# One hybrid layer on one core: the RWKV chain's solve taken tokens-first, its rounds regrouped, attention buffers freed sooner, x loaded in longer rows

## The chip, the cores and the metric

The kernel runs on one core of a Trainium2 chip. The metric is the device time of one execution in microseconds (us), the median of several runs. A profile is one further execution, recorded instruction by instruction.

## What is computed

The reference is one layer of a hybrid network on 256 tokens of width 2048, all in float32:

```python
h = rms_norm(x, norm_g)
proj = h @ w_in                      # 2048 -> 20672 columns, cut into the parts below
y_a = attention(q_a, k_a, v_a, rel_bias) * silu(z_a)         # 12 heads of 128, causal, T5 bias
y_b = rwkv7_time_mix(r_b, k_b, v_b, lw, la, ...) * silu(z_b) # 24 heads of 64
y_c = memory_cross_attention(q_c, mem_n, w_mem_kv) * silu(z_c)
merged = g_a*(y_a @ w_proj_a) + g_b*(y_b @ w_proj_b) + g_c*(y_c @ w_proj_c)
out = rms_norm(x + merged @ w_out, final_norm_g)
```

The time mix keeps a 64x64 state per head and steps through the tokens:

```python
sa = einsum('bhvk,bhk->bhv', state, a_t)
state = state * w_t + sa[..., None] * b_t + v_t[..., None] * k_t
y_t = einsum('bhvk,bhk->bhv', state, r_t)
```

The kernel takes it in two chunks of 128 tokens: with the decays folded into the vectors, a chunk needs four 128x128 products of tokens with tokens (its grams, masked), the inverse of a unit triangular 128x128 matrix, and a few small matmuls with the state.

## The kernel before, in words

**The main stream.** The program walks a list of jobs, one per 256 or 512 output columns of a weight matrix. A job is cut into steps of four (or two, for the 512 wide ones) slices of 128 input rows. For each step a 512 KB piece of the weight is loaded into `raw` (`issue_dma`, L259, three buffers, on SP's queue), split into a high and a low part in `wt` by ACT (L270) and DVE (L273), and multiplied on PE: 16 matmuls of 512 and 256 columns (L308, L309) or 12 of 512 columns (L306). These are the main matmuls; their results stand in the four PSUM tiles `pm`.

**The lanes.** All else (the time mix, attention, the norms) is written as generators. After each step of the main stream `step_lanes` lets every lane go on to its next `yield`, so a lane's instructions stand between two steps on every engine, and `yield 2` leaves a step out. Engines execute in this written order. A lane waits for another by `wait(key)`, which only costs it steps. `force(key)` in a job's evacuation, and `drain()` at the end of a phase, run the lanes with no main matmuls between them. Lanes use four other PSUM tiles, `psd`, in turn: a fifth use waits until the first has been read.

**One pair of the time mix.** The 24 heads go in six groups g of four heads. `pairs_lane(g)` computes decay and gate (L521, L528), waits for R and K, builds the vectors `AR` and `BK`, turns sg and R to tokens on PE for the norms (L589), then waits for V and turns V and BK (L601 to L603) into `tok`. It starts `rw_lane(g)`, which computes the grams `GS` in four rounds (L623, masked by DVE at L627 and L628), sends the diagonal blocks through DRAM and back (`d1`, L660 and L669, both on SP's queue), inverts them on DVE (L680, L684), completes the inverse `XF` on PE (L715 to L745), and then for each chunk forms the input `W` of the inverse (`from_v` L640 and L643, `turn_a` L651), applies it (L762), updates the state S (L770, L771) and gives the output YT (L779, L780). The rest of the lane normalises: YT is turned on PE (L791), mean and difference are taken by DVE from PSUM (L794 to L800), and the result Y is turned back (L828).

**Attention A.** `attn_a(g)` loads the bias by way of DRAM rows (`spread_rows`, L421, on ACT's queue: `fr<-fd`), computes scores (L847, L849), the softmax, transposes of it (L876) and the product with V (L883, L885). `keep_evac`, which stores the next pair's q and k, forces the whole of the pair before.

**The start and the joint.** x is loaded in eight pieces of 256 KB on two queues; `x_stats` sums squares of each quarter on ACT and DVE while PE turns the identity (L915). After the last job of the time mix `open_p2` drains the lanes, gives their memory back and loads the second input `mem` (L981).

Of the kernel before, what the change touches and what calls it, by code (L numbers as in the profile page):

```python
# [38 lines left out]
def tile_hybrid(ctx: ExitStack, tc: tile.TileContext, x, mem, rel_bias, norm_g, mem_norm_g, w_in,  # L39
# [443 lines left out]
    def keep_evac(nm, g):  # L483
        def f(_):
            if g:
                force(("attn", g - 1))
# [19 lines left out]
    def pairs_lane(g):  # L506
# [17 lines left out]
        yield 1  # L524
# [58 lines left out]
        yield 1  # L583
        for t, o in ((sq, nb), (r, bs)):
# [8 lines left out]
        yield 1  # L593
        yield from wait(("V", g))
        yield 1
# [16 lines left out]
    def rw_lane(g, AR, BK, tok, nb, bs, esc):  # L612
        rw, GS, XF, X64 = (E[k] for k in ("rw", "GS", "XF", "X64"))
        if g:
            yield from wait(("state_free", g - 1))
        for c in range(2):
            for q in range(2):

                pv = [ps_side().rearrange("p (w x t) -> p w x t", w=2, x=2) for h in range(2)]
                for w in range(2):  # L620
                    for h in range(2):
                        rows = slice(64 * h, 64 * h + 64)
# [6 lines left out]
                yield 1  # L629
        flags["gram", g] = True  # L630
        S = E["S"]
        halves = [slice(64 * h, 64 * h + 64) for h in range(2)]

        def from_v(c, AY):
# [12 lines left out]

        def turn_a(AY, W):
            p = ps_side()
            for q in range(2):  # L650
                pe.transpose(p[:, q * 128:q * 128 + 128], AY[:, q, 0], ident)  # L651
            act.activation(W[:, 0], p[:, 0:256].rearrange("p (i v) -> p i v", i=4), AF.Copy)
# [6 lines left out]
        for d, s in enumerate(D4):  # L659
            nc.sync.dma_start(d1[d].rearrange("u s t -> s u t"), GS[s, :, 0, s])  # L660
        NB = rw.tile([128, 32, 32], FT, name="NB")
# [9 lines left out]
        for c in range(31, 0, -1):  # L671
# [15 lines left out]
            if c == 16:  # L687

                if g:
                    yield from wait(("pair_free", g - 1))  # L690
                AY0 = rw.tile([128, 2, 2, 128], FT, name="AY0", tag="Yq")
                from_v(0, AY0)
            if c == 8:
                W = rw.tile([128, 2, 4, 64], FT, name="W")
                turn_a(AY0, W)
# [23 lines left out]
        for s in D4[0:2]:  # L719
            act.activation(X64[s, :, s], XN[s], AF.Copy)  # L720
        yield 1
# [26 lines left out]

        Tt = rw.tile([128, 2, 2, 2, 128], FT, name="Tt", tag="NB")
        AY1, YT = Tt[:, 0], Tt[:, 1]  # L750
        for c in range(2):
            AY = (AY0, AY1)[c]
            if c:
                from_v(1, AY)
                yield 1
                W = rw.tile([128, 2, 4, 64], FT, name="W")
                turn_a(AY, W)
# [31 lines left out]
        for c in range(2):  # L789
            for q in range(2):  # L790
                pe.transpose(p[:, c * 256 + q * 128:c * 256 + q * 128 + 128], YT[:, c, q], ident)  # L791
# [516 lines left out]
```

## Time and profile before

| what | value |
|---|---|
| median of 3 runs | 1486.32 us (1486.04 to 1487.34) |
| the profiled execution's own time | 1486.92 us |
| its span, first to last instruction | 1485.2 us |
| PE busy over the span | 1453.7 us, 98% |
| DVE, ACT, POOL busy | 64%, 51%, 12% |
| PE busy in 0 to 40 us | 30.90 us |
| PE busy in 700 to 800 us | 93.01 us |
| PE busy in 1400 to 1485 us | 77.31 us |

The span is 1.7 us shorter than the execution's own time, which has the launch around it. Matmuls overlap in the pipeline, so a matmul's own duration is longer than the distance to the next start; what a group costs is read from start to start, or from the group's busy time. "Idle before" is the time in which an engine had nothing in flight, with what ended it.

### The profile page before, as it was taken

What the parts mean: (1) busy time and instruction counts of PE and PEld (TensorE: products, weight loads), DVE (VectorE), ACT (ScalarE), POOL (GpSimd) and SP (SyncE); (2) the same over time, 40 slices, a digit from 0 to 9 for tenths busy, and PEclk for the clock granted to TensorE, in tenths of its full rate; (3) what the DMA queues carried; (4) which work ended last, traced back from release to release, by engine and by line L of the source; (5) the groups of instructions that cost most, each with busy time, mean ns of one, the idle gap of its engine ahead of it and who ended that gap; (6) DMA issues with size and microseconds to landing.
All of it is one profiled execution on the core that took longest, in us unless ns stands there. A gap on an engine that the chain in (4) does not pass through costs nothing.

```text
span 1485.2 us, 22008 instructions
## 1 busy us (share of the span) xinstructions
PE 1453.7 (98%) x8219; PEld 1212.2 (82%) x8219; DVE 944.5 (64%) x1871; ACT 752.4 (51%) x1127; POOL 179.9 (12%) x252
## 2 busy tenths in 40 slices
PE   7999999999999999999899999999999999999997
PEld 6877878888888888788688888888888888888887
DVE  5667678687787688694557555655545545544555
ACT  6535545556456456455655545544443443444443
POOL 5211201313212224102100000000000000000011
PEclk9999999999999999999999999999999999999999
DMA  6655556456555465466556555566555565555753
GB/s 178 182 166 165 161 151 173 144 149 177 145 168 167 133 181 169 136 174 181 143 172 197 169 171 164 166 198 195 185 190 192 185 194 189 186 196 186 266 196 133
DMA packets 208544, 258.88 MB, mean 174 GB/s; under 512 B 28236, under 2 KB 146660, under 8 KB 207796
## 3 DMA queue, kind: packets, MB, share of 16 engines
q1 hardware_dynamic: 202160, 247.11, 54.4%
q10 hardware_dynamic: 4452, 6.71, 1.3%
q0 software_dynamic: 1824, 3.65, 0.9%
q8 instruction: 65, 1.06, 0.3%
q14 instruction: 43, 0.35, 0.1%
HBM read 253.74 MB, written 6.05 MB: 175 GB/s over the span
## 4 chain that ended last, share of the span: by engine, by line
PE 85%; DVE 5%; DMA 4%; ACT 3%; issue 1%; SPq 1%; POOL 0%; ACTq 0%; DVEq 0%; POOLq 0%
PE pm L306 43%; PE pm L308 22%; PE pm L309 11%; DMA raw<-in_w_in_dram 3%; DVE wt L273 2%; PE psd L623 2%; DVE fs_t L680 1%; ACT wt L270 1%; DVE X L684 1%; PE psd L1047 1%; PE psd L762 1%; PE psd L643 1%; PE psd L154 1%; PE psd L739 0%; DMA x_sb<-in_x_dram 0%
## 5 line engine op out<-in xcount | busy, mean ns | idle before, releaser
L273 DVE TENSOR_TENSOR wt<-raw,wt 128x1024 fp32r<-128x1024 f32 (+1 forms) x451 | 557.8, 1238 | 417.1 <-ACT wt L270 416.1
L270 ACT ACTIVATE wt<-raw 128x1024 fp32r<-128x1024 f32 (+1 forms) x452 | 477.0, 1056 | 491.3 <-PE pm L306 274.4
L308 PE MATMUL pm<-hT,wt 128*128 128x512 f32 (+1 forms) x1632 | 594.0, 405 | 0.0
L309 PE MATMUL pm<-hT,wt 128*128 128x256 f32 (+1 forms) x1632 | 458.9, 281 | 2.8 <-DVE wt L273 2.8
L308 PEld LDWEIGHTS pm<-hT,wt 128*128 128x128 f32 (+1 forms) x1632 | 307.2, 188 | 81.0 <-issue 6.9
L306 PE MATMUL pm<-wt,hT 128*128 128x512 f32 x1440 | 335.6, 391 | 0.0
L306 PEld LDWEIGHTS pm<-wt,hT 128*128 128x128 f32 x1440 | 268.5, 188 | 59.0 <-issue 2.6
L309 PEld LDWEIGHTS pm<-hT,wt 128*128 128x128 f32 (+1 forms) x1632 | 309.0, 189 | 4.4 <-DVE wt L273 4.1
L306 PE MATMUL pm<-wt,mg 128*128 128x512 f32 (+1 forms) x384 | 79.3, 367 | 0.0
L306 PEld LDWEIGHTS pm<-wt,mg 128*128 128x128 f32 x384 | 65.7, 189 | 12.5
L1193 POOL MEMSET sso<- 128x16 f32 x1 | 0.1, 117 | 612.0 <-PE pm L306 612.0
L680 DVE TENSOR_TENSOR fs_t<-X,NB 128x30 f32<-128x30 f32 (+13 forms) x354 | 65.1, 223 | 13.3 <-POOL zsa L323 7.6
L317 ACT ACTIVATE et<-pm 128x256 f32<-128x256 f32 (+1 forms) x112 | 42.8, 383 | 53.3 <-PE pm L309 46.6
L306 PE MATMUL pm<-wt,yas 128*128 128x512 f32 x288 | 67.6, 395 | 0.0
L306 PE MATMUL pm<-wt,ybs 128*128 128x512 f32 x288 | 67.6, 395 | 0.0
L306 PEld LDWEIGHTS pm<-wt,ybs 128*128 128x128 f32 x288 | 54.3, 188 | 12.6
L306 PEld LDWEIGHTS pm<-wt,yas 128*128 128x128 f32 x288 | 54.3, 188 | 12.7
L323 POOL TENSOR_TENSOR lraw<-lraw,et 128x256 f32<-128x256 f32 (+1 forms) x38 | 43.9, 1176 | 133.7 <-ACT lraw L322 133.7
L684 DVE TENSOR_TENSOR X<-X,fs_t 128x30 f32<-128x30 f32 (+13 forms) x354 | 55.5, 192 | 0.6
L306 PE MATMUL pm<-wt,mT 128*128 128x512 f32 x192 | 45.8, 395 | 0.0
L308 PE MATMUL pm<-mT,wt 128*128 128x512 f32 x128 | 45.4, 395 | 0.0
L306 PE MATMUL pm<-wt,ycs 128*128 128x512 f32 x192 | 45.3, 395 | 0.0
(302 smaller groups left out, 1304.8 us busy)
## 6 DMA issues: line engine op xcount, KB each, us to landing
raw<-in_w_in_dram SPq DMA_DIRECT2D x320, 512.0 KB, 3.6
raw<-in_w_mem_kv_dram SPq DMA_DIRECT2D x32, 512.0 KB, 3.9
raw<-in_w_out_dram SPq DMA_DIRECT2D x32, 512.0 KB, 4.6
raw<-in_w_proj_a_dram SPq DMA_DIRECT2D x24, 512.0 KB, 3.5
raw<-in_w_proj_b_dram SPq DMA_DIRECT2D x24, 512.0 KB, 3.6
raw<-in_w_proj_c_dram SPq DMA_DIRECT2D x16, 512.0 KB, 4.2
NB<-d SPq DMA_DIRECT2D x24, 128.0 KB, 3.8
fr<-fd ACTq DMA_DIRECT2D x6, 385.0 KB
```

The lines of the kernel that those rows point to most:

```text
L154: pe.transpose(pv[:, a, t], src[:, t, (k + a) * 128:(k + a + 1) * 128], ident)
L270: act.activation(w[:, :, 0], r, AF.Copy)
L273: eng.tensor_tensor(w[:, :, 1], r, w[:, :, 0].bitcast(FT), OP.subtract)
L306: pe.matmul(ps[:, 0:j.n], l, r, start=first and n == 0, stop=last and n == 2)
L308: pe.matmul(ps[0:j.m], hi, both, start=first, stop=last, skip_group_check=True)
L309: pe.matmul(ps[0:j.m, 256:512], lo, top, start=False, stop=last, skip_group_check=True)
L317: act.activation(t, ps[0:j.m, 256:512], AF.Copy)
L323: pool.tensor_tensor(j.dst[f], j.dst[f], t, OP.add)
L623: pe.matmul(pv[h][:, w].rearrange("p x t -> p (x t)"), BK[rows, q, c, w * 128:(w + 1) * 128], AR[rows, q, c].rearrange("p x t -> p (x t)") ...
L643: pe.matmul(pv[rows, q], tok[:, q, c, rows], GS[:, c * 4 + 2 * q + h, 2:4].rearrange("p x t -> p (x t)"), start=(c == 0), stop=True, skip_ ...
L680: dve.tensor_tensor(t, X[:, k0:8, c:c + 1].to_broadcast([128, m, hi - lo]), NB[:, lo:hi, c].rearrange("p (o n) -> p o n", o=1).to_broadcas ...
L684: dve.tensor_tensor(X[:, k0:8, lo:hi], X[:, k0:8, lo:hi], t, OP.add)
```

## The change

Six things are changed.

1. In `rw_lane` the input W of the inverse is computed with tokens on the partitions at once: the gram is the stationary operand and `tok` the moving one (64 columns). The turn (`turn_a`) and the feature-first copy AY are gone. The part of the output that AY carried is added in PSUM to YT's own matmuls, and YT leaves PSUM by ACT (before: an add by DVE).
2. The grams of a chunk (both q) stand in one round of eight matmuls, where there were two rounds of four; `from_v(0)` moves behind the inversion on DVE.
3. The grams of chunk 0 wait only for chunk 0 of the pair before (`half_free`), those of chunk 1 for the whole pair.
4. In `pairs_lane` one `yield` is taken out and the wait for V moves ahead of the turns of sg and R, so all turns stand in one step.
5. `keep_evac` forces only the scores of the pair before; `attn_a` waits by itself until the pair before has turned its softmax. Q and K of the last pair come ahead of the last two V and Z jobs.
6. x is loaded in four pieces of 512 KB (4 KB rows), and the squares are summed over halves; the turn of `prow1` stands after 11 warming turns, where it stood after 9.

```diff
-    for h in range(4):
+    for h in range(2):
         for t in range(2):
-            cs = slice(h * D // 4, (h + 1) * D // 4)
+            cs = slice(h * D // 2, (h + 1) * D // 2)
             (nc.scalar if t else nc.sync).dma_start(x_sb[:, t, cs], xv[:, t, cs])
...
             if g:
-                force(("attn", g - 1))
+                force(("scores", g - 1))
             t = E["rw"].tile([128, 2, 256], FT, name=nm)
...
+        yield from wait(("V", g))
+        yield 1
         for t, o in ((sq, nb), (r, bs)):
...
-        yield 1
-        yield from wait(("V", g))
-        yield 1
         v = St.pop(("V", g))
...
-        if g:
-            yield from wait(("state_free", g - 1))
         for c in range(2):
+            if g:
+                yield from wait((("half_free", "state_free")[c], g - 1))
             for q in range(2):
...
-                yield 1
+            yield 1
...
+        def from_v(c):
+
+            W = rw.tile([128, 2, 4, 64], FT, name="W")
             p = ps_side()
-            pv = p.rearrange("p (q n) -> p q n", q=2)
+            pv = p[:, 0:256].rearrange("p (i v) -> p i v", i=4)
             for q in range(2):
                 if c:
-                    pe.matmul(pv[:, q], S[:, q], AR[:, q, 1].rearrange("p x t -> p (x t)"), start=True, stop=False,
+                    pe.matmul(p[:, q * 128:q * 128 + 128], AR[:, q, 1, 0], S[:, q], start=True, stop=False,
                               skip_group_check=True)
                 for h, rows in enumerate(halves):
-                    pe.matmul(pv[rows, q], tok[:, q, c, rows],
-                              GS[:, c * 4 + 2 * q + h, 2:4].rearrange("p x t -> p (x t)"), start=(c == 0), stop=True,
+                    pe.matmul(pv[:, 2 * q + h], GS[:, c * 4 + 2 * q + h, 2], tok[:, q, c, rows], start=(c == 0), stop=True,
                               skip_group_check=True)
-            act.activation(AY, p.rearrange("p (q x t) -> p q x t", q=2, x=2), AF.Copy)
...
+            act.activation(W[:, 0], pv, AF.Copy)
+            return W
...
             for q in range(2):
+                if c:
+                    pe.matmul(pv[:, q], S[:, q], AR[:, q, 1, 1], start=True, stop=False, skip_group_check=True)
                 for h, rows in enumerate(halves):
-                    pe.matmul(pv[rows, q], W[:, 1, 2 * q + h], GS[:, c * 4 + 2 * q + h, 1], start=True, stop=True)
-            dve.tensor_tensor(YT[:, c], pv, AY[:, :, 1], OP.add)
+                    u = c * 4 + 2 * q + h
+                    pe.matmul(pv[rows, q], tok[:, q, c, rows], GS[:, u, 3], start=(c == 0), stop=False,
+                              skip_group_check=True)
+                    pe.matmul(pv[rows, q], W[:, 1, 2 * q + h], GS[:, u, 1], start=False, stop=True,
+                              skip_group_check=True)
+            act.activation(YT[:, c], pv, AF.Copy)
+            if c == 0:
+                flags["half_free", g] = True
...
+        if g:
+            yield from wait(("soft", g - 1))
...
-    AJ = AJ[0:3] + VJ[0:1] + AJ[3:8] + VJ[1:2] + AJ[8:14] + VJ[2:3] + AJ[14:18]
+    AJ = AJ[0:3] + VJ[0:1] + AJ[3:8] + VJ[1:2] + AJ[8:14] + AJ[15:17] + VJ[2:3] + [AJ[14], AJ[17]]
```

The lines of the changed kernel are some ten lower: its gram is L622, the turn of YT L780, the turn of Y L817, the turns in `pairs_lane` L590 and L599 to L601, the stores and loads of `d1` L652 and L663.

**The joint, on PE.** The last turns and products of the lanes (`psd`) among main matmuls (`pm`), where the phase of the time mix ends. Before:

```order
L309 MATMUL pm<-hT,wt 128x256
L876 MATMUL psd<-ident,as 128x128 x6
L883 MATMUL psd<-pT,va 128x256
L885 MATMUL psd<-pT,va 128x128
L883 MATMUL psd<-pT,va 128x256
L885 MATMUL psd<-pT,va 128x128
L828 MATMUL psd<-ident,Y 128x128 x4
L308 MATMUL pm<-hT,wt 128x512
```

In the changed kernel the last lane work on PE in that phase is this:

```order
L308 MATMUL pm<-hT,wt 128x512
L309 MATMUL pm<-hT,wt 128x256
L817 MATMUL psd<-ident,Y 128x128 x4
L308 MATMUL pm<-hT,wt 128x512
L309 MATMUL pm<-hT,wt 128x256
```

Before, attention's turns and products and the turn of Y stand behind each other with no main matmul between them. Now the turn of Y stands alone between two steps, 176 main matmuls ahead of the first turn of `mem` (160 lie between the joint and that turn before), and attention's end is further up.

**The turns of pair 1, on PE.** The piece from the turns of sg and R to those of V and BK, while pair 0 finishes. Before:

```order
L589 MATMUL psd<-ident,sg 128x128 x4
L589 MATMUL psd<-ident,R 128x128 x4
L306 MATMUL pm<-wt,hT 128x512 x12
L651 MATMUL psd<-ident,Tt 128x128 x2
L306 MATMUL pm<-wt,hT 128x512 x12
L762 MATMUL psd<-W,XF 128x64 x4
L601 MATMUL psd<-ident,V 128x128 x2
L602 MATMUL psd<-ident,BK 128x128
L603 MATMUL psd<-ident,BK 128x128
L601 MATMUL psd<-ident,V 128x128 x2
L602 MATMUL psd<-ident,BK 128x128
L603 MATMUL psd<-ident,BK 128x128
```

And in the changed kernel:

```order
L306 MATMUL pm<-wt,hT 128x512 x24
L780 MATMUL psd<-ident,YT 128x128 x4
L590 MATMUL psd<-ident,sg 128x128 x4
L590 MATMUL psd<-ident,R 128x128 x4
L599 MATMUL psd<-ident,V 128x128 x2
L600 MATMUL psd<-ident,BK 128x128
L601 MATMUL psd<-ident,BK 128x128
L599 MATMUL psd<-ident,V 128x128 x2
L600 MATMUL psd<-ident,BK 128x128
L601 MATMUL psd<-ident,BK 128x128
L306 MATMUL pm<-wt,hT 128x512 x12
L622 MATMUL psd<-AR,BK 128x256 x8
```

The turn of YT of the pair before and all turns of this pair now stand in one step: five `psd` tiles in a row, where the step holds four. The same piece stands there for pairs 1 to 5.

**The blocks' way through DRAM, on SP's queue.** The first weight loads (L259), the stores of pair 0's diagonal blocks and their loads. Before:

```order
L259 DMA raw<-in_w_in_dram 128x4x256 x26
L660 DMA d_1009<-GS 32x8x32 x4
L259 DMA raw<-in_w_in_dram 128x4x256
L669 DMA NB<-d_1009 32x1024 x4
L259 DMA raw<-in_w_in_dram 128x4x256 x9
```

And in the changed kernel:

```order
L259 DMA raw<-in_w_in_dram 128x4x256 x24
L652 DMA d_951<-GS 32x8x32 x4
L259 DMA raw<-in_w_in_dram 128x4x256
L663 DMA NB<-d_951 32x1024 x4
L259 DMA raw<-in_w_in_dram 128x4x256 x9
```

The stores and loads of the blocks come two weight loads earlier. The bias rows of pair 1 (`fr<-fd`) keep their place on ACT's queue, behind the first K job.

## Rows read from the trace of the kernel before

**Rows 1.** The page's first part: busy us, share of the span, instructions.

```profile
PE 1453.7 (98%) x8219; PEld 1212.2 (82%) x8219; DVE 944.5 (64%) x1871; ACT 752.4 (51%) x1127; POOL 179.9 (12%) x252
```

**Rows 2.** Waits of PE: who was waited for, us in total, times, longest us.

```profile
PE psd L828 <- DVE Y L820: 4.9, 1, 4.9
PE psd L883 <- ACT pT L877: 2.9, 3, 2.1
PE pm L309 <- DVE wt L273: 2.8, 3, 1.9
PE psd L601 <- DVE V L431: 1.3, 1, 1.3
```

**Rows 3.** Timeline of PE at the joint: start us, us, instruction, idle before.

```profile
733.47 0.81 PE L876 MATMUL psd<-ident,as 128*128 128x128 f32 x6
736.37 0.70 PE L883 MATMUL psd<-pT,va 128*128 128x256 f32 x2 [2.08 <-ACT pT L877]
...
743.43 1.09 PE L828 MATMUL psd<-ident,Y 128*128 128x128 f32 x4 [4.91 <-DVE Y L820]
744.17 0.78 PE L308 MATMUL pm<-hT,wt 128*128 128x512 f32 x1
```

**Rows 4.** Busy time by stretch: length, busy us of engines, PEclk, DMA share, GB/s.

```profile
744.20:747.50 3.30, 3.30 (x13) 2.82 (x12) 0.87 (x2) 0.00 (x0) 0.00 (x0) 0.51 0.33 55
747.50:750.80 3.30, 3.30 (x21) 2.91 (x20) 0.97 (x1) 1.06 (x1) 0.00 (x0) 1.00 0.95 382
...
119.40:122.80 3.40, 3.40 (x12) 2.92 (x12) 3.40 (x22) 1.65 (x5) 0.00 (x0) 0.50 0.53 154
```

**Rows 5.** Timeline of PE at its longest wait inside the phase.

```profile
119.19 0.42 PE L309 MATMUL pm<-hT,wt 128*128 128x256 f32 x1 [1.94 <-DVE wt L273]
```

**Rows 6.** Waits of SP's queue: who was waited for, us, times, longest.

```profile
SPq L669 <- DMA d<-GS: 15.9, 10, 7.5
...
SPq L981 <- DVE yb L831: 6.0, 1, 6.0
```

**Rows 7.** Timeline of ACT's queue ahead of that wait of PE.

```profile
98.93 0.61 ACTq L421 DMA_DIRECT2D fr<-fd  x1
```

**Rows 8.** PE's groups by line and shape: count, busy us, mean ns, idle before.

```profile
L643 PE MATMUL psd<-GS,tok 128*64 128x256 f32 x96 | 14.3, 398 | 0.0
L762 PE MATMUL psd<-W,XF 128*128 128x64 f32 x96 | 12.0, 268 | 0.0
...
L779 PE MATMUL psd<-GS,W 128*64 128x128 f32 x96 | 7.9, 279 | 0.0
...
L640 PE MATMUL psd<-AR,S 128*128 128x256 f32 x24 | 7.8, 404 | 0.0
...
L849 PE MATMUL psd<-ka,qa 128*128 128x128 f32 x24 | 3.6, 274 | 0.0
...
L651 PE MATMUL psd<-ident,Tt 128*128 128x128 f32 x12 | 2.3, 272 | 0.0
```

**Rows 9.** Timeline of PE at turns of pair 1 and of YT.

```profile
178.14 0.66 PE L589 MATMUL psd<-ident,sg 128*128 128x128 f32 x4
...
178.98 2.99 PE L306 MATMUL pm<-wt,hT 128*128 128x512 f32 x12
...
196.84 0.60 PE L791 MATMUL psd<-ident,Tt 128*128 128x128 f32 x4
197.37 1.13 PE L623 MATMUL psd<-AR,BK 64*128 64x256 f32 x8
```

**Rows 10.** Timeline of DVE reading the turned YT from PSUM.

```profile
197.48 0.69 DVE L794 TENSOR_REDUCE gn_m<-psd 128x8 f32<-128x512 f32 x1 [0.73 <-PE psd L791]
...
198.41 0.69 DVE L800 TENSOR_TENSOR Y<-psd,gn_m 128x512 f32<-128x512 f32 x1
```

**Rows 11.** DVE: a group of the splits, and the timeline at the start.

```profile
L273 DVE TENSOR_TENSOR wt<-raw,wt 128x1024 fp32r<-128x1024 f32 x448 | 554.9, 1240 | 417.1 <-ACT wt L270 416.1 <-ACT et L317 0.2
...
10.09 0.69 DVE L905 SCALAR_TENSOR_TENSOR nt_scr<-x_sb 128x512 f32<-128x512 f32 x1 [0.23 <-DMA x_sb<-in_x_dram]
```

More of the change, by code (lines that the diff above doesn't have):

```diff
@@ L613, in rw_lane @@
         rw, GS, XF, X64 = (E[k] for k in ("rw", "GS", "XF", "X64"))
-        if g:
-            yield from wait(("state_free", g - 1))
+        S = E["S"]
+        halves = [slice(64 * h, 64 * h + 64) for h in range(2)]
         for c in range(2):
+            if g:
+                yield from wait((("half_free", "state_free")[c], g - 1))
             for q in range(2):
@@ L620, in rw_lane @@
                 for w in range(2):
-                    for h in range(2):
-                        rows = slice(64 * h, 64 * h + 64)
+                    for h, rows in enumerate(halves):
                         pe.matmul(pv[h][:, w].rearrange("p x t -> p (x t)"), BK[rows, q, c, w * 128:(w + 1) * 128],
@@ L660, in rw_lane @@
             nc.sync.dma_start(d1[d].rearrange("u s t -> s u t"), GS[s, :, 0, s])
+        if g:
+            yield from wait(("turned", g - 1))
         NB = rw.tile([128, 32, 32], FT, name="NB")
@@ L686, in rw_lane @@
                 yield 1
[L687 to L695, printed above, removed]
         for r, s in enumerate(D4):
@@ L720, in rw_lane @@
             act.activation(X64[s, :, s], XN[s], AF.Copy)
+        W = from_v(0)
         yield 1
@@ L747, in rw_lane @@
         yield 1
-        Tt = rw.tile([128, 2, 2, 2, 128], FT, name="Tt", tag="NB")
-        AY1, YT = Tt[:, 0], Tt[:, 1]
+        YT = rw.tile([128, 2, 2, 128], FT, name="YT", tag="NB")
         for c in range(2):
-            AY = (AY0, AY1)[c]
             if c:
[L754 to L757, printed above, removed]
+                W = from_v(1)
                 yield 1
@@ L791, in rw_lane @@
                 pe.transpose(p[:, c * 256 + q * 128:c * 256 + q * 128 + 128], YT[:, c, q], ident)
+        flags["turned", g] = True
         py = p.rearrange("p (u v) -> p u v", u=8)
@@ L820, in rw_lane @@
         dve.tensor_tensor(Y, Y, Yq, OP.add)
-        flags["pair_free", g] = True
         yield 2
@@ L843, in attn_a @@
         yield from wait(("qa", g), ("ka", g))
+        if g:
+            yield from wait(("soft", g - 1))
         q, k = St[("qa", g)], St[("ka", g)]
@@ L849, in attn_a @@
             pe.matmul(p0_[:, h * 128:h * 128 + 128], q[:, h, 0:128], k[:, h, 0:128], start=True, stop=True)
+        flags["scores", g] = True
         s = rw.tile([128, 2, 384], FT, name="as")
@@ L877, in attn_a @@
             act.activation(pT[:, h], p[:, 0:384], AF.Copy)
+        flags["soft", g] = True
         yield 1
@@ L897, in x_stats @@
     def x_stats():
-        scr = xp.tile([128, 2, D // 4], FT, name="nt_scr")
-        sp = stat.tile([128, 2, 4], FT, name="x_sp")
-        for h in range(4):
-            for t, eng in ((0, act), (1, dve)):
-                q, o, acc = x_sb[:, t, h * 512:h * 512 + 512], scr[:, t], sp[:, t, h:h + 1]
-                if t:
-                    dve.scalar_tensor_tensor(o, q, 1.0, q, op0=OP.mult, op1=OP.mult, accum_out=acc)
-                else:
-                    act.activation(o, q, AF.Square, accum_out=acc)
-            if h > 1:
-                issue_dma(nc.scalar)
+        scr = xp.tile([128, 2, D // 2], FT, name="nt_scr")
+        sp = stat.tile([128, 2, 2], FT, name="x_sp")
+        for h in range(2):
+            cs = slice(h * D // 2, (h + 1) * D // 2)
+            act.activation(scr[:, 0], x_sb[:, 0, cs], AF.Square, accum_out=sp[:, 0, h:h + 1])
+            dve.scalar_tensor_tensor(scr[:, 1], x_sb[:, 1, cs], 1.0, x_sb[:, 1, cs], op0=OP.mult, op1=OP.mult,
+                                     accum_out=sp[:, 1, h:h + 1])
+            issue_dma(nc.scalar)
         p = ps_side()
-        pe.transpose(p[:, 0:128], x_sb[:, 0, 1024:1152], ident)
+        pe.transpose(p[:, 0:128], x_sb[:, 0, 0:128], ident)
         for i in range(18):
-            if i == 9:
+            if i == 11:
                 turn_params(prow1, "1", 16)
```

9 lines of the change are left out of this document (removed).

## The prediction

> **What bounds the kernel now.** I read the page's busy times first. PE is busy for 1453.7 us, 98% of the span, DVE for 64% and ACT for 51% [rows 1]. So DVE's and ACT's sums cannot set the time; a change pays where it shortens PE's own work, or where PE stands still. The second view is therefore the list of PE's waits, and in it the longest ones [rows 2]: 4.9 us for the last Y of the time mix, 2.9 us in three places for attention's transposed softmax, 2.8 us for split weights, 1.3 us for V. The third view is the timeline at the largest of them, the joint behind the time mix [rows 3]: attention's turns begin at 733.47 us, PE waits 2.08 and 4.91 us in turn, and the next main matmul starts at 744.17. Fourth I read stretches behind waits. After the joint, 13 main matmuls fit in 3.30 us where 21 fit in the next 3.30, and PEclk reads 0.51 and 1.00: TensorE came out of the joint at 1.2 GHz and went back to 2.4 [rows 4]. So a long wait costs more than its own length. The same stands behind a wait inside the phase: PE waits 1.94 us for split weights until 119.19 [rows 5] and the next 3.40 us hold 12 matmuls at a PEclk of 0.50 [rows 4].
>
> **The joint (changes 3, 4 and 5).** Before, the last pair of the time mix and the last attention end with no main matmul beside them. In the new order the turn of Y stands between two steps of the main stream and attention's products lie further up; PE has no lane work left at the joint. What goes: the waits, 2.08 + 4.91 = 6.99 us [rows 3]; the slow main matmuls behind them, 3.30 x (1 - 13/21) = 1.26 us [rows 4]; and the slow turn of Y, 744.17 - 743.43 = 0.74 us where the same four turns take 197.37 - 196.84 = 0.53 [rows 3, 9], 0.2 us. The turns and products themselves stay, elsewhere. I take -8.4 us. The other end is -2.4, under the second rival.
>
> **The starved weights at 119 us (changes 2 and 3).** SP's queue issues weight loads and the blocks' loads in one order. It waited up to 7.5 us at the blocks' loads for the stores to land [rows 6]; weights behind it came late. ACT's queue had issued bias rows at 98.93 us [rows 7], beside those stores. The grams now take two steps less, so the stores go out two weight loads earlier, ahead of the bias rows. The wait is worth 1.94 us [rows 5] plus the slow stretch behind it: 12 matmuls in 3.40 us, where 21 in 3.30 make 21.6 in 3.40, so 3.40 x (1 - 12/21.6) = 1.5 us [rows 4]. The ends are 0 and -3.5. I take -3.0, near the full end, since a landing that no longer meets the rows should not hold SP so long; the weights' own loads still meet them, which keeps it from being all.
>
> **V's turn (change 4).** PE waited 1.3 us for V in pair 0 [rows 2]. The eight turns of sg and R, 178.98 - 178.14 = 0.84 us [rows 9], now stand between the same release and V's turn and fill that much of it: -0.8 us, ends 0 and -1.3.
>
> **Attention let go at its scores (change 5).** The waits for the transposed softmax come to 2.9 us, 2.1 of them at the joint and counted; 0.8 is left in two places [rows 2]. One is in a forced pair of steps, which the change no longer forces. I take -0.4 us, ends 0 and -0.8. What stands behind the new wait in `attn_a` is only that lane; it has steps in hand.
>
> **PE's own work (change 1).** A float32 matmul shows as two instructions. Over the six pairs the rows give for what goes or is replaced: L643 14.3, L640 7.8, the turns 2 x 2.3 (two equal groups), L779 7.9, in sum 34.6 us [rows 8]. For the new: the grams as stationary operand with 64 moving columns are like L762, the same 96 instructions, 12.0 us; the two products with S, 24 instructions of 128 columns each, like L849, 2 x 3.6; YT's two sets like L779, 2 x 7.9. The sum is 35.0, so +0.4 us. Ends: the narrow set at half of L762's price, 6.0, or at what it replaces, 14.3, which is -5.6 to +2.7. I keep L762, the same shape. The Trainium skill ("TensorE: Matmul & The Clock Gate", section on LDWEIGHTS) says that a weight load takes its number of columns over 1.2 in ns, however few columns move. That speaks against narrow moving operands under 128 columns of weights; by it 96 loads take an estimated 10.2 us and the sum would be 1.8 us lower. L762's 12.0/96 = 125 ns agrees in kind. DVE's add of YT and ACT's copy of AY and turned W change places with other ACT copies; both engines have room [rows 1] and I cost them at nothing. If their room goes, the next late thing is a split weight.
>
> **Five PSUM tiles in one step (change 4).** This is what the change adds. For pairs 1 to 5, the turn of YT and four more turns stand in one step, and the fifth tile is the first again. PE comes to it 0.53 us for YT's turns, 0.84 for sg and R and about half of that again, 0.42, for the first tile of V and BK: 1.8 us after the step's start at 196.84 in the rows' scale [rows 9]. DVE has read YT's tile when L800 ends, 198.41 + 0.69 = 199.10, 2.26 us after it [rows 10]. So PE waits about 0.5 us each time if DVE is free, and up to 1.24 us more if a split stands ahead [rows 11]. Five steps: +2.4 us, ends 0 and +8.5. I take the free end, since DVE waited 0.73 us for those turns in the row [rows 10]. Behind the waiting PE stand only main matmuls whose weights are split three steps ahead.
>
> **The start (change 6).** The last square began at 10.09 us, after a wait of 0.23 for x, and took 0.69 for 512 columns [rows 11]. A half has 1024; a DVE operation on 1024 takes 1.24 [rows 11], so the sums end 0.55 us later if x lands at the same time, and earlier if longer rows land faster. No row prices a 4 KB row; I take 0, ends +0.55 and, as likely, -0.55. The Trainium skill ("Perfetto Trace Analysis", section on DMA optimizations) has both: larger pieces use the memory's bandwidth better, and splitting lets some start sooner. The second speaks against this part, and the wait of 0.23 for the last piece shows the loads as the limit then, which is the case of the first; by the second the sum would be 0.55 us higher.
>
> **The sum.** -8.4 - 3.0 - 0.8 - 0.4 + 0.4 + 2.4 + 0 = -9.8 us. The profiled execution took 1486.92 us, so 1477.1; the median of the runs, 1486.32, is 0.6 lower, so **1476.5 us**. About 0.2% (3 us) is what can be told from no change.
>
> **The rivals.**
>
> *The five steps make it slower.* The mechanism is the fifth PSUM tile, in the step that turns YT, sg, R, V and BK. Without its +2.4 the sum is -12.2. It is slower by 3 us when the five steps cost 15.2 us, 3 us each. A wait that long would be followed by the lower clock, as those of 1.94 and 4.91 us were [rows 3 to 5], so the price goes to 3 + 1.5 each, some 23 us, and the time to 1486.3 - 12.2 + 23 = 1497 us. For it: DVE also carries two reductions and four scalings of that step. Against: the longest queue that I find there is 0.5 + 1.24. Chance 0.05.
>
> *The joint keeps a wait of another kind.* SP waited 6.0 us at the joint before it could load `mem` [rows 6], and that load stands ahead of weights on SP. PE no longer pauses meanwhile. If weights run out, up to 6.0 us comes back: 1476.5 + 6.0 = 1482.5. For it: SP's order is not changed. Against: PE had no wait of this kind behind the joint, though the load was issued in that place [rows 2]. Chance 0.13.
>
> *The regrouping does not cure the starved weights.* Bias rows now meet the blocks' loads and the weights in place of the stores, and the wait moves but stays: 1476.5 + 3.0 = 1479.5. Chance 0.2.
>
> *Both of these, or one with the dear end of the five steps*: within 3 us of before, about 1485. Chance 0.07.
>
> **How the numbers follow.** My forecast has 0.55. Faster by over 0.2% are the forecast and the second and third rival, which with a little of the last make 0.89; within it 0.07; slower the first, 0.04 of its 0.05. The range goes down by the ends of the forecast's own terms taken together in part (-0.5 for weights, -0.5 for V, -0.4 for attention, -2.4 for the five steps, and about half of the 5.6 on PE's work, 2.8): 1476.5 - 6.6, near 1470, and up to the second rival, 1482.5. Some 2 in 10 are left out.
>
> **What would show it.** Right: no waits of PE of 2 us or more between 700 and 760 us and PEclk of 1.00 there; the wait for split weights near 115 us gone or short; in the steps of pairs 1 to 5 a wait of about half a microsecond in the turns of V and BK, released by DVE's L800 of before; PE's groups for `from_v` and YT in sum within a few us of 35. Wrong: a new wait at the joint released by a weight load; waits of 2 us or more behind the turns, with the lower clock after them; the start's first main matmul over 1 us later.

## The result and the profile after

The changed kernel takes 1478.93 us (median of 5 runs, 1477.08 to 1480.51); the kernel before, run beside it, 1486.32 us (5 runs). The ratio is 0.9948, 95% interval 0.9935 to 0.9961: 7.4 us faster. The forecast was 1476.5 us, its range 1470 to 1482.5. The profiled execution took 1478.29 us, its span is 1476.5.

First the page's first part of the kernel after (as [rows 1]), and then its list of PE's waits (as [rows 2]): who was waited for, us in total, times, longest.

```profile
PE 1449.2 (98%) x8315; PEld 1222.3 (83%) x8315; DVE 946.2 (64%) x1855; ACT 747.3 (51%) x1122; POOL 181.8 (12%) x252
```

```profile
PE pm L309 <- DVE wt L273: 3.4, 5, 0.9
PE psd L599 <- DVE Y L790: 3.4, 5, 0.9
...
PE psd L622 <- DVE GS L627: 2.3, 4, 0.6
```

PE is busy 4.5 us less. The waits for Y, V and attention's softmax that led [rows 2] are gone or below half a microsecond; two new groups stand in the list, 3.4 us at the turns of V and 2.3 us inside the gram rounds.

The joint, as stretches of the kernel after (length, busy us of PE, PEld, DVE, ACT and POOL, PEclk, DMA share, GB/s):

```profile
700.00:730.00 30.00, 30.00 (x183) 25.85 (x182) 18.84 (x25) 17.83 (x25) 5.82 (x5) 1.00 0.47 138
730.00:760.00 30.00, 30.00 (x173) 26.07 (x172) 18.16 (x23) 16.46 (x25) 1.47 (x2) 1.00 0.79 249
```

No idle and a full clock through the joint, where [rows 3, 4] had 6.99 us of waits and 3.3 us at 0.51. The turn of Y stands between two steps of the main stream, in PE's timeline:

```profile
733.08 0.60 PE L817 MATMUL psd<-ident,Y 128*128 128x128 f32 x4
```

The place of the starved weights, in PE's timeline of the kernel after and as a stretch (as [rows 5] and the last of [rows 4]):

```profile
122.94 0.39 PE L309 MATMUL pm<-hT,wt 128*128 128x256 f32 x1 [0.76 <-DVE wt L273]
...
126.57 0.38 PE L309 MATMUL pm<-hT,wt 128*128 128x256 f32 x1 [0.54 <-DVE wt L273]
...
130.52 0.39 PE L309 MATMUL pm<-hT,wt 128*128 128x256 f32 x1 [0.86 <-DVE wt L273]
```

```profile
119.40:122.80 3.40, 2.78 (x17) 2.13 (x16) 1.95 (x8) 3.39 (x5) 0.00 (x0) 1.00 0.50 152
```

One wait of 1.94 us with the lower clock behind it has become three of 0.54 to 0.86 at the full clock. The blocks' loads on SP's queue no longer wait 7.5 us (as the first of [rows 6]):

```profile
SPq L663 <- DMA d<-GS: 8.9, 9, 1.9
```

Weights are still late at one place: ACT stands 6.49 us without a landed one. PE does not wait there, and its three waits have another source. For the first, ACT's split stands behind attention's softmax (L861), which itself waited for DVE; three splits in a row follow. ACT's timeline of the kernel after:

```profile
107.04 1.06 ACT L270 ACTIVATE wt<-raw 128x1024 fp32r<-128x1024 f32 x1 [6.49 <-DMA raw<-in_w_in_dram]
...
117.24 1.50 ACT L861 ACTIVATE as<-as,asm 128x256 f32<-128x256 f32 x4 [2.55 <-DVE asm L857]
...
120.58 2.94 ACT L270 ACTIVATE wt<-raw 128x1024 fp32r<-128x1024 f32 x3
```

For the other two the split waits on DVE, which works without a gap: the inversion of the blocks (L674, L678) stands there between its splits. As stretches of the kernel after (columns as above, DVE is the third busy time):

```profile
122.80:126.20 3.40, 3.09 (x16) 2.45 (x16) 3.40 (x19) 1.43 (x4) 0.00 (x0) 1.00 0.53 154
126.20:129.60 3.40, 3.03 (x16) 2.44 (x16) 3.40 (x18) 2.73 (x6) 2.66 (x5) 1.00 0.54 158
```

The two new groups of waits, in PE's timeline at pair 4, and DVE's last reading of YT's tile:

```profile
492.74 0.60 PE L780 MATMUL psd<-ident,YT 128*128 128x128 f32 x4
493.18 0.60 PE L590 MATMUL psd<-ident,sg 128*128 128x128 f32 x4
493.62 0.60 PE L590 MATMUL psd<-ident,R 128*128 128x128 f32 x4
495.15 0.41 PE L599 MATMUL psd<-ident,V 128*128 128x128 f32 x2 [0.93 <-DVE Y L790]
...
499.02 1.56 PE L622 MATMUL psd<-AR,BK 64*128 64x256 f32 x10
501.15 1.10 PE L622 MATMUL psd<-AR,BK 64*128 64x256 f32 x6 [0.57 <-DVE GS L627]
```

```profile
494.31 0.69 DVE L790 TENSOR_TENSOR Y<-psd,gn_m 128x512 f32<-128x512 f32 x1
```

DVE has read YT's tile at 494.31 + 0.69 = 495.00 us, 2.26 us after the step's first turn, and only then can PE write the fifth one. Five such waits, 0.50 us in three pairs and 0.93 in two, make the 3.4. In these last two pairs the gram rounds that follow wait as well, since only three of the four `psd` tiles are there: attention's product of pair 2 was finished at 427.3 us, and DVE takes it out of PSUM, multiplied with its gate, at 513.7. Both rows are of the kernel after, from PE's and DVE's timelines:

```profile
426.96 0.38 PE L878 MATMUL psd<-pT,va 128*128 128x128 f32 x2
```

```profile
513.70 0.68 DVE L881 TENSOR_TENSOR ya<-psd,zsa 128x512 f32<-128x512 f32 x1
```

PE's own work, from its groups after (line, form, count, busy us, mean ns, idle before), which answer to [rows 8]:

```profile
L641 PE MATMUL psd<-tok,GS 128*128 128x64 f32 x96 | 13.3, 271 | 0.0
...
L763 PE MATMUL psd<-GS,tok 128*64 128x128 f32 x96 | 10.6, 286 | 0.0
L765 PE MATMUL psd<-GS,W 128*64 128x128 f32 x96 | 10.0, 273 | 0.0
...
L760 PE MATMUL psd<-AR,S 128*128 128x128 f32 x24 | 5.2, 299 | 0.0
L638 PE MATMUL psd<-S,AR 128*128 128x128 f32 x24 | 4.9, 287 | 0.0
```

Their sum is 44.0 us, 9.4 more than the 34.6 of [rows 8] that they replace; the time that they take out of the main stream is another matter, and the last experiments are about it.

**Where the time came from.** Matched by the count of main matmuls, number 3200 (behind the joint) starts at 773.86 us before and at 764.97 after: 8.89 us. At the last main matmul the distance is 8.86. So nothing behind the joint changed, and the whole gain is in the phase of the time mix. There, between the first main matmul and number 3200 (8.7 us less), PE's waits went from 14.1 to 9.4 us and the main matmuls' loss at the lower clock from 3.1 to 0. The lanes' groups cost 161.7 us before and 159.2 after, waits taken off: 142.4 and 145.2 in their own distances from start to start, 19.3 and 13.9 at their edges, which is what the main matmul right ahead of a group and the one right behind take beyond their usual 117 to 233 ns. The rest, +1.6 us, is spread over the other main matmuls in small amounts.

### The profile page after: what moved, and what is told of

It reads as the page before. It is cut to its first block, busy times and chain, and to the rows that moved or that the text cites. A ratio compares the mean times of both kernels' runs of the same rounds, so it can differ in the third digit from the quotient of the medians.

```text
span 1476.5 us, 22151 instructions
## 1 busy us (share of the span) xinstructions
PE 1449.2 (98%) x8315; PEld 1222.3 (83%) x8315; DVE 946.2 (64%) x1855; ACT 747.3 (51%) x1122; POOL 181.8 (12%) x252
## 4 chain that ended last, share of the span: by engine, by line
PE 89%; DVE 4%; DMA 2%; ACT 1%; issue 1%; POOL 1%; SPq 0%; ACTq 0%; DVEq 0%
PE pm L306 43%; PE pm L308 24%; PE pm L309 12%; PE psd L622 2%; DVE wt L273 1%; DMA raw<-in_w_in_dram 1%; DVE fs_t L674 1%; PE psd L641 1%; PE psd L1037 1%; PE psd L743 1%; DMA NB<-d 1%; PE psd L154 1%; DMA x_sb<-in_x_dram 1%; ACT wt L270 1%; DVE X L678 1%
## 5 line engine op out<-in xcount | busy, mean ns | idle before, releaser
L308 PE MATMUL pm<-hT,wt 128*128 128x512 f32 (+1 forms) x1632 | 587.1, 402 | 0.0
L674 DVE TENSOR_TENSOR fs_t<-X,NB 128x30 f32<-128x30 f32 (+13 forms) x354 | 64.9, 223 | 7.5 <-DMA NB<-d 7.1
L678 DVE TENSOR_TENSOR X<-X,fs_t 128x30 f32<-128x30 f32 (+13 forms) x354 | 56.3, 194 | 0.6
```

Of the source, the lines that this page charges most:

```text
L308: pe.matmul(ps[0:j.m], hi, both, start=first, stop=last, skip_group_check=True)
L674: dve.tensor_tensor(t, X[:, k0:8, c:c + 1].to_broadcast([128, m, hi - lo]), NB[:, lo:hi, c].rearrange("p (o n) -> p o n", o=1).to_broadcas ...
L678: dve.tensor_tensor(X[:, k0:8, lo:hi], X[:, k0:8, lo:hi], t, OP.add)
```

## The experiments

Twelve kernels were run, each beside runs of the kernel before on its chip.

**Change 5 alone, put into the kernel before.**

```diff
-                force(("attn", g - 1))
+                force(("scores", g - 1))
...
+        if g:
+            yield from wait(("soft", g - 1))
...
-    AJ = AJ[0:3] + VJ[0:1] + AJ[3:8] + VJ[1:2] + AJ[8:14] + VJ[2:3] + AJ[14:18]
+    AJ = AJ[0:3] + VJ[0:1] + AJ[3:8] + VJ[1:2] + AJ[8:14] + AJ[15:17] + VJ[2:3] + [AJ[14], AJ[17]]
```

> The kernel before with change 5 alone (scores forced, softmax waited for, Q and K of the last pair ahead of V and Z). Theory, the joint needs both chains to end early: attention's 2.08 us wait goes, but the turn of Y still stands at the joint, behind the chain through DVE and ACT that ran beside attention before; PE then waits 6 to 9 us for Y and comes back at the lower clock. Time 1484 to 1487 us, so no change to -2. Rival, attention alone made the joint late: no wait of PE over 1 us there, 1478 us (-8.4).

Measured: 1488.84 us against 1487.85, ratio 1.0007 (0.9998 to 1.0017): no difference. PE's waits and a stretch of that kernel:

```profile
PE psd L828 <- DVE Y L820: 9.0, 1, 9.0
```

```profile
741.50:751.80 10.30, 5.82 (x20) 5.09 (x21) 5.67 (x12) 0.63 (x1) 1.33 (x1) 0.50 0.42 121
```

Attention is out of the joint, and the time mix's wait there grows from 4.91 to 9.0 us: it fills what attention left. The chain that ends at Y set the joint.

**All but change 5.** The same lines turned back in the changed kernel.

> The changed kernel without change 5 (attention of the pair before forced whole, old order of the last jobs). Theory, both chains: Y is early, attention's end stands at the joint alone; PE waits about 2 us for the transposed softmax there, then some at the lower clock, and the waits for the softmax inside the phase (0.8 us) come back: 1482 us, 3 above the changed kernel. Rival, the time mix alone made the joint late: 1479 us, as the changed kernel.

Measured: 1485.44 against 1487.85, ratio 0.9981 (0.9971 to 0.9991). PE's timeline at the joint, and the stretch around it:

```profile
742.65 0.70 PE L872 MATMUL psd<-pT,va 128*128 128x256 f32 x2 [0.48 <-ACT pT L866]
```

```profile
700.00:760.00 60.00, 59.52 (x358) 51.84 (x357) 33.56 (x43) 36.12 (x63) 9.89 (x11) 1.00 0.65 198
```

At the joint attention costs 0.48 us and no lower clock, not 2.08: with the time mix out of the way its softmax is nearly done. Yet without change 5 some 5 us of the gain are missing (2.4 us against 7.4). The list of PE's waits has 4.1 of it inside the phase: 2.3 more for split weights than in the change, and 1.8 in a gram round, which waits until DVE has read attention's scores. One wait of 1.09 us for a split weight, at 333.64, follows where the evacuation of q and k has forced attention's steps and DVE has two steps' work of the inversion between two splits. Another of 1.12, at 117.20, stands in pair 0, where nothing is forced yet. So the forced steps account for a part, and the rest stays open.

```profile
PE pm L309 <- DVE wt L273: 5.7, 9, 1.1
...
PE psd L622 <- DVE as L842: 1.8, 1, 1.8
```

So neither half does it alone: about -2.4 us without change 5, +1 (no difference) with it alone, -7.4 together.

**The product tile freed at once.** In the changed kernel ACT copies attention's product out of PSUM when it is done, and the gate is multiplied in place later.

```diff
+        yg = ya[:, 2 * g:2 * g + 2]
+        act.activation(yg, two(p), AF.Copy)
...
-        dve.tensor_tensor(ya[:, 2 * g:2 * g + 2], two(p), St[("zsa", g)], OP.mult)
+        dve.tensor_tensor(yg, yg, St[("zsa", g)], OP.mult)
```

> The changed kernel, attention's product copied out of PSUM by ACT at once (into ya, multiplied by silu in place later), so that its PSUM tile is not held until Z of that pair is there. Theory, a held tile: in the changed kernel the product of pair 2 is read 87 us after it was made and that of pair 3 64 us after, and the grams of pairs 4 and 5 have three tiles for rounds of four. The four waits of PE in the grams (2.3 us, with the restart some 3.2) go, and the waits at V's turn of pairs 4 and 5 fall from 0.9 to 0.5 us: 1475 us, 3 to 4 below the changed kernel. Rival, DVE is too slow for a round of eight: the waits stay, 1479 us.

Measured: 1475.95 against 1487.85, ratio 0.9915 (0.9900 to 0.9930). The gram rounds' waits for the mask are gone from PE's list, and those of the fifth tile are 0.5 us at most:

```profile
PE psd L599 <- DVE Y L790: 2.5, 5, 0.5
```

That is some 5 us less than the change by the two ratios (0.9948 and 0.9915, whose intervals do not meet), 3.0 by the two medians; the waits that went come to 3.2 (2.3 and 0.9). Others came in the profiled execution (0.6 more for split weights, 1.7 at L700, L838 and L622), so PE's idle time fell by only 0.8 there. The held tile is the cause of the gram waits; what they were worth is less sure.

**The turns in two steps.** One `yield 1` back between the turns of sg and R and those of V and BK. (The whole change also took out a `yield 1` between decay and gate, L521 and L528; that one stays out.)

```diff
         dve.reciprocal(nb, nb)
+        yield 1
```

> The changed kernel with one more step between the turns of sg and R and those of V and BK. Theory, five tiles in a step: the five waits at V's turn (3.4 us) go; five more groups of lane work on PE cost 0.17 us each on entry and exit (from the changed kernel's shorter sum of entries and exits): 1478.9 - 3.4 + 0.9 = 1476.4 us. Rival, the waits come from the chain through DVE and only move to the grams: 1479 us, with more than 2.3 us of waits at the grams.

Measured: 1475.42 against 1487.85, ratio 0.9911 (0.9894 to 0.9927). No wait at the turns of V is left in PE's list; the gram waits stay, and split weights are later:

```profile
PE pm L309 <- DVE wt L273: 5.4, 8, 1.1
...
PE psd L623 <- DVE GS L628: 2.3, 4, 0.6
```

So putting five tiles in one step was a loss: the wait for V that it was to fill is gone without it.

**Both of the last two.**

> The changed kernel with both repairs: attention's product copied out of PSUM at once, and one more step between the turns of sg and R and those of V and BK. Theory, two causes of waits that don't depend on each other: 3.0 us (tile held) and 3.5 us (five tiles) below the changed kernel, 1472.5 us, with no wait over 0.3 us at the grams or at V's turn. Rival, both take the same time off the same late DVE: 1475.5 us, as either alone.

Measured: 1474.12 (1473.02 to 1475.20) against 1486.83, ratio 0.9913 (0.9897 to 0.9928), the shortest median of the study. PE's waits in the phase are then nearly all split weights:

```profile
PE pm L309 <- DVE wt L273: 6.4, 11, 1.1
```

The median lies between the theory's 1472.5 us and the rival's 1475.5. The two gains do not add up: by the medians 3.0 and 3.5 us less than the change, and 4.8 together; by the ratios the three are the same. What PE no longer waits for in PSUM it waits for in part at the splits (6.4 us, where the change has 3.4).

**x as before, in eight pieces.** Change 6 undone in the changed kernel.

```diff
-    for h in range(2):
+    for h in range(4):
...
-            cs = slice(h * D // 2, (h + 1) * D // 2)
+            cs = slice(h * D // 4, (h + 1) * D // 4)
```

> The changed kernel with x in eight pieces and squares over quarters, as before. Theory, the start is worth nothing either way: first main matmul within 0.5 us of the changed kernel's 16.5 us, time 1479 us. Rival by longer rows: it starts 0.5 to 1 us later. Rival by smaller pieces: 0.5 us earlier.

Measured: 1478.54 against 1486.83, ratio 0.9938 (0.9923 to 0.9954), beside 0.9948: the start is worth nothing that can be told. The first main matmul starts at 15.52 us in this profile, at 16.54 in the change's, and between 16.0 and 16.9 in those of the other kernels made from the changed one, whose loading of x is the same. The two other kernels with eight pieces have 16.72 (before) and 15.88 (change 5 alone), so it may come earlier, by less than 1 us, and nothing of that is left at the end.

**Grams in four rounds again.** Change 2 undone in part: a step after each q.

```diff
-            yield 1
+                yield 1
```

> The changed kernel with the grams of a chunk in two rounds of four again. Theory, the round of eight pays only by fewer groups of lane work on PE and loses by the held tile: the four waits at the grams (2.3 us, 3.2 with the restart) go, and each added group costs 0.17 us: 1476.5 us. Rival, the round of eight is what made the chain short enough: a wait of PE comes back at the joint, over 1481 us.

Measured: 1483.05 against 1486.83, ratio 0.9968 (0.9958 to 0.9978), 4 us slower than the change, as the rival had it; but not in the rival's place. Between 700 and 770 us PE is busy 69.43 of 70 us at the full clock. The starved weights are back instead, in PE's timeline and as a stretch:

```profile
118.23 0.58 PE L309 MATMUL pm<-hT,wt 128*128 128x256 f32 x1 [2.56 <-DVE wt L273]
```

```profile
117.90:121.30 3.40, 3.07 (x10) 2.68 (x11) 3.40 (x21) 1.12 (x4) 0.00 (x0) 0.50 0.53 148
```

```profile
PE pm L309 <- DVE wt L273: 9.2, 9, 2.6
...
SPq L663 <- DMA d<-GS: 9.6, 5, 4.7
```

The waits for split weights are 5.8 us longer than in the change (of their 9.2, 2.6 are this wait and 4.4 are five waits between 549 and 662 us, which were not followed up), the waits for PSUM (5.7) are gone, and the lower clock takes 2.5. That is the change's second part, told from its absence: one round for a chunk sends the blocks off earlier (their first store is issued at 92.19 us in the change, at 97.97 here and at 99.29 before), and that is what takes the long wait and the lower clock away.

**The bias rows of pair 1 later**, in the changed kernel.

```diff
-            later(4, spread_rows, g + 1)
+            later(4 if g else 20, spread_rows, g + 1)
```

> The changed kernel with the bias rows of pair 1 written 16 steps later. Theory, those rows hold up weights: the three waits for split weights at 121 to 131 us (2.2 us) go, 1476.5 us. Rival, the inversion on DVE and what waits for it on ACT hold up the splits: the waits stay, 1479 us.

Measured: 1479.35 against 1486.83, ratio 0.9949 (0.9932 to 0.9966): no different from the change. PE's timeline has two of the three waits left, and one of 0.48 us at 665.66 with 3.4 us of lower clock behind it that the change does not have.

```profile
124.64 0.39 PE L309 MATMUL pm<-hT,wt 128*128 128x256 f32 x1 [0.38 <-DVE wt L273]
...
128.59 0.38 PE L309 MATMUL pm<-hT,wt 128*128 128x256 f32 x1 [0.86 <-DVE wt L273]
```

ACT's waits for landed weights, which come to 8.1 us between 90 and 120 us in the change, are gone: the split that waited 6.49 us there stands earlier here and behind something else.

```profile
103.62 1.06 ACT L270 ACTIVATE wt<-raw 128x1024 fp32r<-128x1024 f32 x1 [3.07 <-DVE as L845]
```

So the bias rows were what made those weights land late, but they are at most a part (some 0.9 us) of PE's waits. The rest is the rival's: the splits stand behind the inversion on DVE, as DVE's full stretches from 122.80 us in the kernel after show, and the time did not move.

**What it costs PE to go to a lane and back.** By the list of starts, the first main matmul behind a lane's group takes 0.08 to 0.1 us more than the next, and up to main matmul 3200 the change has 99 groups where the kernel before had 129. To see whether a group as such costs something, 96 more turns of the identity stand in the projections of the third phase, one in each of 96 steps or four in each fourth. Their results are used nowhere.

```diff
+        if i0 + 30 <= i < i0 + 126 and (True):
+            p = ps_side()
+            for k in range(1):
+                pe.transpose(p[:, k * 128:k * 128 + 128], ident, ident)
```

The second kernel has `(i - i0) % 4 == 3` for `True` and `range(4)`.

> The changed kernel with 96 extra turns of the identity on PE, into PSUM tiles that nobody reads, one in each of 96 steps of the projections. The same work as its twin, in 96 groups. Theory, a group of lane work costs at its entry and exit whatever it holds: about 0.1 us for each of 72 more groups, 6 to 7 us over the twin. Rival, only the work counts: the same time as the twin.

> The changed kernel with the same 96 extra turns of the identity, four in each fourth step, 24 groups. Theory: 6 to 7 us below its twin. Rival: the same time as the twin. Either way about 10 us of work (96 turns at about 0.1 us) over the changed kernel.

Measured: 1492.07 against 1492.95 us, ratios 1.0037 (1.0025 to 1.0049) and 1.0040 (1.0025 to 1.0054). The same: 72 groups fewer save nothing, and the theory of a price for each group falls. The profiled spans differ by 3.9 us, but 3.7 of that lie ahead of the first added turn. PE's timeline of the single turns:

```profile
1026.50 0.27 PE L1271 MATMUL psd<-ident 128*128 128x128 f32 x1
1026.53 2.98 PE L306 MATMUL pm<-wt,hT 128*128 128x512 f32 x12
1029.35 0.27 PE L1271 MATMUL psd<-ident 128*128 128x128 f32 x1
```

The main matmul starts 0.03 us after a single turn and the next one then waits for it: the 0.09 us behind a group are the turn's own time, counted one place later.

**The same with products on half of the array.** Sorted by what a group begins with, the trace of before shows another border: the main matmul ahead of a group on the whole array (128 rows, 128 columns) is 4 ns longer than else, the one ahead of a group on 64 or 32 rows or columns 92 ns. So the 96 turns were replaced by 96 products with 64 rows of weights.

```diff
-                pe.transpose(p[:, k * 128:k * 128 + 128], ident, ident)
+                pe.matmul(p[:, k * 128:k * 128 + 128], ident[0:64, :], ident[0:64, :], start=True, stop=True)
```

> The changed kernel with 96 more products in the projections of the third phase, one in each of 96 successive steps, each with 64 rows of the identity as weights (64 x 128) and 128 moving columns, so that it stands on half of TensorE's array; their results go nowhere. Theory (the main matmul ahead of a product on part of the array is some 0.09 us longer, and the one behind it some 0.02 longer than behind a whole one, whatever stands in between): each of the 96 pays its own time, about 0.11 us, and 0.11 us more for the change to and fro, together 0.22 us each, 21 us: about 1500 us. Rival (no such price; what the list of entries shows belongs to those lanes' own work): as the turns of the identity, about 0.12 us each, 11 to 13 us: about 1491 us.

> As the run before it, but four products in each fourth step. Theory: the change to and fro is paid 24 times, not 96: 96 x 0.11 + 24 x 0.11 = 13 us, about 1492 us, some 8 us under the single ones. Rival: the same time as the single ones, within 1 us, as the turns showed.

Measured: 1540.64 us single and 1510.28 in fours, ratios 1.0352 (1.0337 to 1.0368) and 1.0157 (1.0140 to 1.0174). 30.4 us apart over 72 groups: 0.42 us for each change to half of the array and back. The theory holds in kind, and its price is nearly four times the 0.11 that the entries had told. PE's timelines, single and in fours:

```profile
1024.86 0.48 PE L1271 MATMUL psd<-ident 64*128 64x128 f32 x2
1025.27 3.02 PE L306 MATMUL pm<-wt,hT 128*128 128x512 f32 x12
1028.21 0.48 PE L1271 MATMUL psd<-ident 64*128 64x128 f32 x2
```

```profile
1035.24 1.16 PE L1271 MATMUL psd<-ident 64*128 64x128 f32 x8
1036.33 10.03 PE L306 MATMUL pm<-wt,ycs 128*128 128x512 f32 x42
```

A step of 12 main matmuls with one product lasts 1028.21 - 1024.86 = 3.35 us; with one whole turn it lasts 1029.35 - 1026.50 = 2.85. One product takes 0.41 us until the next main matmul starts, four take 1.09, so each further one 0.23 (two instructions), and 0.18 of the first is the way back. The rest is not in these rows: the last main matmul ahead is 0.09 us longer, and the first one behind 0.11. It is the part of the array that costs, not a float32 product as such: in the kernel after, the main matmul of 256 columns ahead of products on the whole array (L743, L838, L760) takes 116 to 121 ns, as the 117 elsewhere, and ahead of L622, L713 or L751 it takes 210. The Trainium skill ("TensorEngine Tiling (Array Packing)", section on Key Properties) says that changing the tiling mode drains TensorE, without a price. The runs agree in that the change costs time; that a drain is what costs it they do not show.

## Why the prediction was right, and where it was not

**The joint: right, -8.8 where -8.4 was forecast.** Waits of 6.99 us, the slow main matmuls and the slow turn of Y are gone, and nothing took their place: PE is never idle from 700 to 760 us. The forecast read attention's 2.08 us there as a wait of its own, which it was not once the time mix was out (0.48, all but change 5), but the sum is the same, since both went. The rest is a reading: of the 13 records that it took for main matmuls [rows 4], three are turns of Y. Ten main matmuls took 3.33 us from start to start there, which is 1.6 more than at the full clock, where the forecast had 1.26. That SP's load of `mem` would bring weights too late there (the second rival) did not happen.

**The starved weights: right in cause, too large.** -3.0 was forecast, "near the full end". The wait of 1.94 and its slow stretch are gone, and the run with four gram rounds shows that the earlier blocks did it. But three waits, 2.16 us together, came in its place, and one of 0.76 at 59 us. All waits for split weights rose from 2.8 to 3.4 us; with the 1.5 of the slow stretch the term is -1.0. The third rival had it that the wait moves but stays, and its time, 1479.5, is nearer to the one measured; but its mechanism is not what kept PE waiting. The bias rows did meet the weights, and with them out of the way two of the three waits stay: the splits stand behind the inversion on DVE. The prediction gave DVE room by its 64% of the whole span; here, for several microseconds, it has none. Its sentence that a split weight is the next late thing if the room goes is what happened.

**V's turn: -1.3 instead of -0.8**; the wait is gone wholly, in the run with the turns in two steps too. There a whole step stands ahead of V's turn, so whether the eight turns fill the wait, as forecast, is not told apart from the place to which the wait for V moved. **Attention let go: -0.4 in its waits**, as forecast: 0.8 went, 0.4 came at L700. What the change buys inside the phase (some 5 us by the second run) does not show as a gain over before. That it keeps the tightened lanes from forced steps is argued, and shown in part. The prediction did not see it.

**PE's own work: the term failed by its size.** Forecast +0.4, with ends of -5.6 and +2.7. From start to start, edges included, the lanes' groups take 2.5 us less, 0.2 of it the slow turn that the joint counts: -2.3, inside the ends but of the other sign. Of the signs of being right this is the one that did not come: the groups' busy times make 44.0 us, not about 35, and by them the change should have cost 9.4 us. Two things part the 9.4 from the -2.3. From start to start the groups that went and those in their place take 29.0 and 30.7 us, +1.7 only: the busy times of neighbours overlap. And the edges of all groups fell by 5.4 us (19.3 to 13.9), which busy times leave out; other lanes rose by 1.1. The edges hold the change between the whole array and a part of it: from_v before went from S's product (whole) to the gram's (64 columns of weights) and back, and every gram round stood by itself. Counted by the forms of the instructions, PE goes to a part of the array 79 times before and 55 times after. 24 times 0.39 to 0.42 us would be 9 to 10 us; the edges show 5.4, with the way back, which lies in a group's last distance, not told apart. That price was measured for products of 128 columns alone, and the rounds' own share in this kernel was not.

The row below with the one after it gives 142.59 - 141.67 = 0.92 us for eight instructions of L641, 115 ns each, and all 96 are 105 ns apart on average, where the group's busy time has 139. The rule weighed in the prediction, a load of weights takes its columns over 1.2 in ns however few move (the Trainium skill, "TensorE: Matmul & The Clock Gate", section on LDWEIGHTS), fits this better than the busy times did: by it they are an estimated 107 ns.

```profile
141.67 1.10 PE L641 MATMUL psd<-tok,GS 128*128 128x64 f32 x8
142.59 0.48 PE L308 MATMUL pm<-hT,wt 128*128 128x512 f32 x1
```

**Five PSUM tiles: +3.4 instead of +2.4.** Where, how often and by whom was right (L790 is L800 of before). In three pairs the price is 0.50; in two it is 0.93, because of the held tile: with the tile freed all five are 0.5.

**Not in the sum at all: the gram rounds' waits, +2.3.** The prediction said nothing of a round of eight matmuls needing four PSUM tiles at once. With attention's product held in the fourth, it has three. Rounds of four had lived with that. Waits that went were not foreseen either: 1.7 us for ACT's copies in the inversion and 0.5 for R; and the main matmuls' spacing lost 1.6 us.

**The start: 0, as forecast.**

The measured terms: -8.8 - 1.0 - 1.3 - 0.4 - 2.3 + 3.4 + 2.3 - 2.2 + 1.6 = -8.7 us, which is what lies between the first main matmul and number 3200; the profiled executions differ by 8.6. That the forecast's -9.8 came near is in part luck: a gain put too high (starved weights, by 2.0), a price put too low (five tiles, by 1.0) and two losses left out (2.3 and 1.6) were met by gains put too low or left out (PE's own work by 2.7, the waits for copies and R 2.2, V 0.5, the joint 0.4).

## What to carry to other kernels

When two lanes end at one joint, the wait is set by the longer one: taking out the shorter gave nothing (change 5 alone), and with the longer out 0.48 us of the wait was left (all but change 5). A share of busy time over the whole span says nothing of a stretch: DVE's 64% was 100% where the splits came late. Before a step is made to use more PSUM tiles, look for who holds one for a long time: a tile that waits for a late gate takes a quarter of the ring from everybody, and one ACT copy gives it back. And price small matmuls from start to start, with the changes between whole and partial array in mind: put products on 64 or 32 rows or columns next to each other, in few rounds.

## What the runs showed of the hardware that was not expected

Going from main matmuls on the whole array to one float32 product on 64 rows and back costs 0.39 us in the profile (from start to start: 0.61 us for a group of one product, 1.29 for four, so 0.22 for each) and 0.42 us by the medians, beyond the product's own time; for turns on the whole array the same reckoning gives under 0.01 us. Single waits of 0.5 us do not always leave the clock alone: a wait of 0.48 us at 665.66 in the run with late bias rows has 10 matmuls at a PEclk of 0.50 behind it, while waits of 0.93 in the kernel after have none. Right ahead of it stand 32 products on 32 rows and 32 columns and eight of 64 columns. In the run with the turns in fours, a wait of 0.30 us at 667.58 behind the same products has a PEclk of 0.51 from 668.7 to 672.1 us. In the kernel after the same products have no wait behind them, and the clock stays at 1.00. The stretch behind the wait at 665.66:

```profile
665.50:668.90 3.40, 3.24 (x10) 2.74 (x11) 2.15 (x3) 3.27 (x8) 3.27 (x7) 0.50 0.60 168
```
